# Weight sums by accumulating DMAs, activation sums on VectorE, and block products that alternate with tiles, in a two-layer Mamba-2 / HGRN2 trunk

## The chip, the cores and the metric

The kernel runs on one core of one Trainium2 chip. The metric is the device time of one execution in microseconds (us). PE is the matrix engine TensorE (PEld its weight loads), DVE is VectorE, ACT is ScalarE, POOL is GpSimd, and SP is SyncE, whose queue issues the DMAs.

## The reference, cut to what matters

Two layers work on 512 tokens of width 1024 in fp32. Each layer has a token mixer (Mamba-2 SSD in layer 0, HGRN2 in layer 1), a squared-ReLU MLP of width 4096, two layer norms and a gated per-layer embedding. The change lies in the MLPs.

```python
def sq_relu_mlp(h, w1, w2):
    a = jax.nn.relu(h @ w1)
    return (a * a) @ w2

for i in range(DEPTH):                                   # DEPTH = 2
    mix = ssd_mixer(x, ...) if i % 2 == 0 else hgrn2_mixer(x, ...)
    h = layer_norm(ALPHA * x + mix, ln_g[i, 0], ln_b[i, 0])
    h = layer_norm(ALPHA * h + sq_relu_mlp(h, w1[i], w2[i]), ln_g[i, 1], ln_b[i, 1])
    x = h + sigmoid(h @ ple_w_gate[i]) * (p[i] @ ple_w_proj[i])
```

Here `h` is 512 x 1024, `w1` 1024 x 4096 and `w2` 4096 x 1024.

## The kernel before

**Precision.** Every large product is made of three matmuls on operands that are split into a high and a low part: `split` makes `whi` on ACT (L110, a cast to fp32r) and `wlo` on DVE (L112, the difference), and `mm3` (L116 to L118) adds high x high, high x low and low x high into one bank. `unit` loads one 128x1024 tile of weights (512 KB) into one of the three `raw` buffers by a DMA on SP's queue and splits it; there are five buffers each for `whi` and `wlo`.

**First half of an MLP.** `hidden(g, p)` makes four tiles of relu(h @ w1)^2, each with one unit of `w1` and 24 matmuls of 512 columns (in the very first four tiles 48 matmuls of 256): ACT takes relu (L369) and square (L370) from the bank. `half_blocks` then prepares half of the blocks of group `g`: the tiles' quarters `a11`, `a12`, `a21`, `a22` and four sums of them, `s1` to `s4`. Seven of these eight are stored as a high part (ACT, L263) and a low part (DVE, L264); the four sums are made on POOL.

**Second half.** The product with `w2` is made by a seven-product scheme for 2 x 2 blocks (Strassen-Winograd) in four groups of 1024 hidden units. `block_product` (`o0` to `o3`) loads the group's eight tiles of `w2` into the buffers `r` (L287), makes eight sums of them on POOL (L290, L292, L321, L325), splits fourteen tiles, and runs seven products of 24 matmuls, each for two row tiles `c`. Products that belong to the same output share a pair of banks (`py0`, `py1` for `x`; two banks `pj` for `y` and `z`): after each product DVE adds the bank into `acc` (L314, L316), and the next product into that bank waits for this.

The order of the pieces is written out by hand:

```python
ORDER = "h00 h01 h10 o0 h11 h20 o1 h21 h30 h31 o2 o3".split()
```

so the last two block products follow each other. In `o3` the next layer norm's chunks (`after(0)` to `after(3)`) are called between the products. The scheduler orders the instructions of each engine by program order and priority when the program is built: `tc.high_priority(offset=SUMS)` moves the loads and sums of `w2` ahead by 220 places, `LEAD` the units by 100. Each engine then runs its list strictly in order.

**Around it.** Ahead of the MLP, `norm` adds the mixer's output into `acc` (L223), normalizes it (L189 to L197) and transposes it on PE (L206). Behind it, the gate takes `h @ ple_w_gate` and `p @ ple_w_proj` per row tile, with a sigmoid buffer `sg` (L410 to L414).

Of the kernel before, what the change touches and what calls it, by code (L numbers as in the profile page):

```python
# [26 lines left out]
LEAD = 100  # L27
RAWS = 3
FIRST = 1000

ORDER = "h00 h01 h10 o0 h11 h20 o1 h21 h30 h31 o2 o3".split()
SUMS = 220

JOBS = "q2 q3 v1 q4 q5 v2 q6 q7 v3 o".split()
FILL = (2.0, 1.0, 1.3, 1.6, 2.3, 2.8)
# [7 lines left out]
def trunk(ctx: ExitStack, tc, a):  # L43
    nc = tc.nc
    pool = lambda name, bufs, **kw: ctx.enter_context(tc.tile_pool(name=name, bufs=bufs, **kw))
    cpool = pool("consts", 1)
    raws = pool("raws", RAWS)
    whip = pool("whip", 5)
    wlop = pool("wlop", 5)
    b8 = pool("b8", 9)  # L50
    accp = pool("accp", 1)
    w4 = pool("w4", 2)
    sm = pool("sm", 2)
    psj = pool("psj", 4, space=PSUM)
    pst = pool("pst", 1, space=PSUM)
    psy = pool("psy", 1, space=PSUM)
# [8 lines left out]
    def mk(p, shape, tag, dt=F32, **kw):  # L65
        return p.tile(list(shape), dt, tag=tag, name=nm(tag), **kw)

    def f32(t):
        return t.bitcast(F32)

    two = dict(xs=2, sz=2, cv=2, cm=2, cbm=2)
    mlp = dict(r=10, blk=2, sg=2)
    bufs = dict(ssd=dict(two, ss=2), mlp0=mlp, hgrn=dict(two, xs=4, sz=4, cv=4, y=2, pv=2, btok=2), mlp1=mlp)
    phase = []

    def begin(name):

        if phase:
            phase[1].__exit__(None, None, None)
            phase.clear()  # L80
        phase.append(tc.tile_pool(name=name, bufs=1, reuse_waits="tile"))
        phase.append(phase[0].__enter__())
        phase.reverse()
        phase.append(bufs[name])

    def tmp(tag, shape, dt=F32):
        return mk(phase[0], shape, tag, dt, bufs=phase[2].get(tag, 1))

    def bank(p, tag):
        return mk(p, [P, T], tag)  # L90
# [8 lines left out]
    def unit(src, lead=LEAD):  # L99
        n = src.shape[1]  # L100
        with tc.high_priority(offset=lead):
            raw = mk(raws, [P, 1024], "raw")
            nc.sync.dma_start(raw[:, :n], src)
        return split(raw[:, :n], lead)

    def split(f, lead=LEAD):
        n = f.shape[1]
        with tc.high_priority(offset=lead):
            hi = mk(whip, [P, 1024], "whi", F32R)
            nc.scalar.copy(hi[:, :n], f)  # L110
            lo = mk(wlop, [P, 1024], "wlo", F32R)
            nc.vector.tensor_sub(lo[:, :n], f, f32(hi[:, :n]))  # L112
        return hi, lo
# [19 lines left out]
    def project(src, xs, ps, m=P, tok=slice(0, T)):  # L133

        hi, lo = src
        for k in range(8):
            c = slice(k * m, (k + 1) * m)
            mm3(ps[:m, tok], hi[:, c], lo[:, c], xs.h(k, tok), xs.l(k, tok), k == 0, k == 7)


    begin("ssd")
    acc = mk(accp, [P, NCH, D], "acc")
    xraw = acc.rearrange("p c (h t) -> p (c h) t", h=2)
# [111 lines left out]

    def half_blocks(blk, z0, z1, p):

        ks = slice(2 * p, 2 * p + 2)
        a11, a12, a21, a22 = z0[:, :, :256], z1[:, :, :256], z0[:, :, 256:], z1[:, :, 256:]

        def put(name, f):
            hi, lo = blk[name][:, 0, ks, :], blk[name][:, 1, ks, :]
            nc.scalar.copy(hi, f)  # L263
            nc.vector.tensor_sub(lo, f, f32(hi))  # L264

        put("a22", a22)
        put("a11", a11)
        put("a12", a12)
        nc.gpsimd.tensor_add(a22, a21, a22)
        put("s1", a22)  # L270
        nc.gpsimd.tensor_sub(a21, a11, a21)
        put("s3", a21)
        nc.gpsimd.tensor_sub(a11, a22, a11)
        put("s2", a11)
        nc.gpsimd.tensor_sub(a12, a12, a11)
        put("s4", a12)

    def block_product(w, blk, first, after=None):


        with tc.high_priority(offset=SUMS):
            raw = {}
            for i, j in ((0, 0), (0, 1), (1, 1), (1, 0)):
                raw[i, j] = []
                for u in range(2):
                    raw[i, j].append(tmp("r", [P, 1024]))
                    nc.sync.dma_start(raw[i, j][u], w[i][j][u])  # L287
            t1, t2, t3, t4 = raw[0, 1], [tmp("r", [P, 1024]) for _ in range(2)], raw[0, 0], raw[1, 0]
            for u in range(2):
                nc.gpsimd.tensor_sub(t1[u], raw[0, 1][u], raw[0, 0][u])  # L290
            for u in range(2):
                nc.gpsimd.tensor_sub(t2[u], raw[1, 1][u], t1[u])  # L292
        seen = set() if first else {(i, j) for i in range(2) for j in range(2)}
        banks = {}

        def product(x, f, name, start, i, j, then=None):
            us = [split(v) for v in f]
            if then is not None:
                with tc.high_priority(offset=LEAD):
                    then()  # L300
            if start:
                banks[name] = [bank(psy, "py%d" % c) if name == "x" else bank(psj, "pj") for c in range(2)]
            t = blk[x]
            for c in range(2):
                ps = banks[name][c]
                sl = slice(c * P, (c + 1) * P)
                for k in range(4):
                    hi, lo = us[k // 2]
                    ks = slice((k % 2) * 512, (k % 2 + 1) * 512)
                    w_ = hi[:, ks], lo[:, ks]  # L310
                    mm3(ps, t[:, 0, k, sl], t[:, 1, k, sl], *w_, start and k == 0, k == 3, skip_group_check=True)
                d = acc[:, 2 * i + c, j * 512 : (j + 1) * 512]
                if (i, j) in seen:
                    nc.vector.tensor_add(d, ps, d)  # L314
                else:
                    nc.vector.scalar_tensor_tensor(d, d, ALPHA, ps, ALU.mult, ALU.add)  # L316
            seen.add((i, j))

        def sums3():
            for u in range(2):  # L320
                nc.gpsimd.tensor_sub(t3[u], t2[u], raw[0, 0][u])  # L321

        def sums4():
            for u in range(2):
                nc.gpsimd.tensor_sub(t4[u], raw[1, 0][u], t2[u])  # L325

        product("a11", raw[0, 0], "x", True, 0, 0, sums3)
        product("a12", raw[1, 0], "z", True, 0, 0, sums4)
        product("s2", t2, "x", False, 1, 0)
        p7 = lambda: product("s3", t3, "y", True, 1, 1)  # L330
        p5 = lambda: product("s1", t1, "x", False, 1, 1)
        p4 = lambda: product("a22", t4, "y", False, 1, 0)
        p3 = lambda: product("s4", raw[1, 1], "x", False, 0, 1)
        if after is None:
            for f in (p7, p5, p4, p3):
                f()
        else:
            p5(), p3(), after(0), after(1)
            p7(), p4(), after(2), after(3)

    def mlp_and_gate(layer, h_s, last):

        w1, w2 = a[f"w1_{layer}"], a[f"w2_{layer}"]
        blocks = {}

        def hidden(g, p):
            if p == 0:
                names = ("a11", "a12", "a22", "s1", "s2", "s3", "s4")
                blocks[g] = {
                    n: tmp("blk", [P, 2, 4, 256], F32R) if n in ("s3", "s4") else mk(b8, [P, 2, 4, 256], "b8", F32R)  # L350
                    for n in names
                }
            tiles = [4 * (2 * g + r) + 2 * p + i for r in range(2) for i in range(2)]
            us = []
            if g == p == 0:
                for m in tiles:
                    us.append((unit(w1[m]), bank(psj, "pj")))
                    project(us[-1][0], h_s, us[-1][1], tok=slice(0, 256))
            zs = []
            for r in range(2):  # L360
                z = mk(w4, [P, 2, T], "ab"[r])
                for i in range(2):
                    if us:
                        u, ps = us[2 * r + i]
                        project(u, h_s, ps, tok=slice(256, 512))
                    else:
                        ps = bank(psj, "pj")
                        project(unit(w1[tiles[2 * r + i]]), h_s, ps)
                    nc.scalar.activation(z[:, i], ps, AF.Relu)  # L369
                nc.scalar.activation(z, z, AF.Square)  # L370
                zs.append(z)
            half_blocks(blocks[g], *zs, p)

        for op in ORDER:
            g = int(op[1])
            if op[0] == "h":
                hidden(g, int(op[2]))
            else:
                if g == 3:
                    h_s, after = norm(2 * layer + 1)  # L380
                w = [[[w2[8 * g + 4 * i + 2 * j + u] for u in range(2)] for j in range(2)] for i in range(2)]
                block_product(w, blocks.pop(g), g == 0, after if g == 3 else None)

        p_s = (mk(w4, [P, 2, T], "a", F32R), mk(w4, [P, 2, T], "b", F32R))
        praw = mk(w4, [P, 2, T], "a")
# [654 lines left out]
```

## Time and profile before

| | |
|---|---|
| time, median of 3 runs (lowest to highest) | 1508.86 us (1508.42 to 1509.92) |
| the profiled execution's own time | 1508.68 us |
| its span, first to last instruction | 1506.9 us |
| mean granted clock of PE | 0.993 |
| busy: PE / DVE / ACT / POOL | 1470.1 / 1101.0 / 723.5 / 274.8 us |
| MLP of layer 0, with gate | about 395 to 810 us of the span |
| MLP of layer 1, with gate | about 1100 us to the end |

A row of the time line reads: start in us from the span's start, duration in us, engine, line, operation, out<-in, shapes, and in brackets how long the engine was idle before it and what ended that wait. A row of a group has behind the bar the busy time in us, the mean duration of one in ns, and the idle time before them. In the rows of stretches, each engine has its busy time and the number of its instructions; behind them stand the granted clock of PE as a share of full speed, the mean busy share of the DMA engines and GB/s. Matmuls are pipelined: a single row's duration is longer than the distance between two starts, and PE's pace is read from the starts.

### The profile page before, as it was taken

Reading aid. Unit: us, or ns where it says so; the run is one execution under the profiler, and the core shown is the slowest. Engines: PE = TensorE matmul, PEld = TensorE weight load, DVE = VectorE, ACT = ScalarE, POOL = GpSimd, SP = SyncE. Lnnn points to the kernel's source line nnn. Section 1 sums busy time; section 2 is a strip of 40 time slices with the busy share of each in tenths; the row PEclk is TensorE's granted clock in tenths of the full one; section 3 lists DMA queues with packets and bytes.
Section 4 is the critical chain, followed back from the end, with each engine's and each line's share of the span. In section 5 each row is a group of like instructions: output and inputs, shape, how many; then the busy total and the mean of one; then the engine's idle time right before and its main releaser. Section 6 shows DMA issues by size and latency. Waiting matters only on the chain.

```text
span 1506.9 us, 19584 instructions
## 1 busy us (share of the span) xinstructions
PE 1470.1 (98%) x7720; PEld 1222.1 (81%) x7720; DVE 1101.0 (73%) x1544; ACT 723.5 (48%) x1020; POOL 274.8 (18%) x136
## 2 busy tenths in 40 slices
PE   8999999999999999998999999999999999999898
PEld 5888888888888888876778998988798888887677
DVE  7998686787777586398944866769766958549883
ACT  6776455563364454453534453543245454444342
POOL 0000000001145251363000000000215435235200
PEclk9999999999999999998999999999999999999999
DMA  6433323234223324130223212222431423314022
GB/s 247 155 112 107 112 93 109 99 118 175 88 69 112 112 89 137 55 126 28 81 70 112 94 61 71 72 70 84 154 112 43 134 90 112 127 42 140 14 85 70
DMA packets 41612, 149.93 MB, mean 99 GB/s; under 512 B 4624, under 2 KB 5136, under 8 KB 41392
## 3 DMA queue, kind: packets, MB, share of 16 engines
q1 hardware_dynamic: 41520, 148.67, 29.4%
q8 instruction: 61, 1.00, 0.3%
q14 instruction: 31, 0.25, 0.1%
HBM read 146.49 MB, written 2.16 MB: 99 GB/s over the span
## 4 chain that ended last, share of the span: by engine, by line
PE 88%; DVE 9%; DMA 2%; ACT 1%; issue 0%; POOL 0%; SPq 0%; ACTq 0%; DVEq 0%
PE pj L116 23%; PE pj L117 23%; PE pj L118 23%; DVE wlo L112 4%; PE py L116 3%; PE py L118 3%; PE py L117 3%; DVE b L264 2%; PE py L778 1%; PE py L587 1%; DVE acc L314 1%; PE pm L557 1%; PE pt L206 1%; PE py L592 1%; DMA a<-in_pT 1%; DVE blk L264 1%
## 5 line engine op out<-in xcount | busy, mean ns | idle before, releaser
L116 PE MATMUL pj<-b,whi 128*128 128x512 f32 (+1 forms) x1024 | 392.0, 383 | 1.2 <-ACT whi L110 1.2
L118 PE MATMUL pj<-b,wlo 128*128 128x512 f32 (+1 forms) x1024 | 388.1, 379 | 0.0
L117 PE MATMUL pj<-b,whi 128*128 128x512 f32 (+1 forms) x1024 | 387.5, 379 | 0.0
L112 DVE TENSOR_TENSOR wlo<-raw,whi 128x1024 fp32r<-128x1024 f32 x180 | 230.4, 1281 | 110.5 <-ACT whi L110 109.6
L110 ACT CAST whi<-raw 128x1024 fp32r<-128x1024 f32 x180 | 188.8, 1050 | 237.3 <-PE pj L117 129.5
L112 DVE TENSOR_TENSOR wlo<-r,whi 128x1024 fp32r<-128x1024 f32 x112 | 194.0, 1737 | 89.7 <-ACT whi L110 89.7
L116 PE MATMUL pj<-whi,b 128*128 128x512 f32 (+1 forms) x712 | 252.3, 355 | 0.5 <-ACT sg L410 0.5
L117 PE MATMUL pj<-wlo,b 128*128 128x512 f32 (+1 forms) x712 | 249.6, 351 | 0.8 <-DVE wlo L112 0.8
L118 PE MATMUL pj<-whi,b 128*128 128x512 f32 (+1 forms) x712 | 250.1, 351 | 0.0
L116 PEld LDWEIGHTS pj<-b,whi 128*128 128x128 f32 x1024 | 192.9, 188 | 36.7 <-ACT whi L110 2.9
L118 PEld LDWEIGHTS pj<-b,wlo 128*128 128x128 f32 x1024 | 192.7, 188 | 35.9 <-DVE wlo L112 1.3
L117 PEld LDWEIGHTS pj<-b,whi 128*128 128x128 f32 x1024 | 192.9, 188 | 34.0 <-issue 1.9
L110 ACT CAST whi<-r 128x1024 fp32r<-128x1024 f32 x112 | 116.8, 1048 | 189.6 <-PE pj L117 60.9
L290 POOL TENSOR_TENSOR r<-r,r 128x1024 f32<-128x1024 f32 x16 | 45.1, 2826 | 767.6 <-DMA r<-in_w 760.0
L117 PEld LDWEIGHTS pj<-wlo,b 128*128 128x128 f32 x712 | 134.7, 189 | 18.4 <-DVE wlo L112 2.0
L116 PEld LDWEIGHTS pj<-whi,b 128*128 128x128 f32 x712 | 134.7, 189 | 17.7 <-ACT sg L410 0.7
L118 PEld LDWEIGHTS pj<-whi,b 128*128 128x128 f32 x712 | 134.5, 189 | 17.0 <-issue 0.2
L116 PE MATMUL py<-whi,b 128*128 128x512 f32 x192 | 77.2, 402 | 15.5 <-DVE acc L314 15.5
L118 PE MATMUL py<-whi,b 128*128 128x512 f32 x224 | 88.8, 398 | 0.0
L264 DVE TENSOR_TENSOR b<-b,b 128x512 fp32r<-128x512 f32 x48 | 62.7, 1322 | 21.5 <-ACT b L263 21.3
L117 PE MATMUL py<-wlo,b 128*128 128x512 f32 x192 | 76.6, 399 | 0.6 <-DVE wlo L112 0.6
L321 POOL TENSOR_TENSOR r<-r,r 128x1024 f32<-128x1024 f32 x16 | 39.8, 2485 | 125.0 <-DVE wlo L112 125.0
(217 smaller groups left out, 2064.3 us busy)
## 6 DMA issues: line engine op xcount, KB each, us to landing
raw<-in_w SPq DMA_DIRECT2D x64, 512.0 KB, 3.6
r<-in_w SPq DMA_DIRECT2D x64, 512.0 KB, 3.7
raw<-in_wssd SPq DMA_DIRECT2D x40, 512.0 KB, 3.6
a<-csd SPq DMA_DIRECT2D x16, 512.0 KB, 3.9
raw<-in_wso SPq DMA_DIRECT2D x16, 512.0 KB, 3.5
raw<-in_wg SPq DMA_DIRECT2D x16, 512.0 KB, 3.6
raw<-in_whvg SPq DMA_DIRECT2D x16, 512.0 KB, 3.5
raw<-in_whq SPq DMA_DIRECT2D x16, 512.0 KB, 3.6
```

Of the source, the lines that this page charges most:

```text
L110: nc.scalar.copy(hi[:, :n], f)
L112: nc.vector.tensor_sub(lo[:, :n], f, f32(hi[:, :n]))
L116: nc.tensor.matmul(out, sh, mh, start=start, stop=False, **kw)
L117: nc.tensor.matmul(out, sh, ml, start=False, stop=False, **kw)
L118: nc.tensor.matmul(out, sl, mh, start=False, stop=stop, **kw)
L206: nc.tensor.transpose(pt[:, j * P : (j + 1) * P], src[:, k * P : (k + 1) * P], ident)
L264: nc.vector.tensor_sub(lo, f, f32(hi))
L290: nc.gpsimd.tensor_sub(t1[u], raw[0, 1][u], raw[0, 0][u])
L314: nc.vector.tensor_add(d, ps, d)
L321: nc.gpsimd.tensor_sub(t3[u], t2[u], raw[0, 0][u])
L557: nc.tensor.matmul(pst_[:, c * P : (c + 1) * P], btok[:, c, :], xw[:, c].rearrange("p h q -> p (h q)"), start=True, stop=True)
L587: nc.tensor.matmul(yd[64 * r : 64 * r + 64, sl], xdt[:, 2 * c + r, :], m[:, r, sl], start=True, stop=True)
```

## The change

The order of the MLP is now written as periods of tiles (T) and products (Q), with the four tiles of `hidden` and the seven products of `block_product` made into generators. Period 0 has eight tiles. In periods 1 to 3 the eight tiles of group `g` alternate with the seven products of group `g - 1`. The last period has the seven products of group 3.

The block sums of `w2` are made by DMAs that add (`accum_op=ALU.add`, issued by POOL, SBUF to SBUF, 512 KB each) on top of a loaded tile; where a negative sign is needed, the tile is loaded into a `raw` buffer and negated on ACT. The three tiles of `w2` that are used unchanged are loaded by `unit`, so that each group has 16 loads on SP's queue where it had 8, and 8 accumulating DMAs where it had 8 sums on POOL. The four sums of activations move to DVE, and the low parts of the half-blocks become scalar-tensor-tensor operations, since two of the blocks are stored with their sign changed. The buffers `sg` go from two to one, POOL's descriptor memory grows from 1024 to 4096 bytes, and a small `pad` tile is added. The matmuls are the same in number and shape.

```diff
-ORDER = "h00 h01 h10 o0 h11 h20 o1 h21 h30 h31 o2 o3".split()
-SUMS = 220
+PERIODS = ("TTTTTTTT",) + 3 * ("TTQTQTQTQTQTQTQ",) + ("QQQQQQQ",)
+SUMS = 300
...
-    mlp = dict(r=10, blk=2, sg=2)
+    mlp = dict(r=10, blk=2)
...
     def half_blocks(blk, z0, z1, p):
...
-        def put(name, f):
+        def put(name, f, sign=1.0):
             hi, lo = blk[name][:, 0, ks, :], blk[name][:, 1, ks, :]
-            nc.scalar.copy(hi, f)
-            nc.vector.tensor_sub(lo, f, f32(hi))
-
-        put("a22", a22)
+            nc.scalar.activation(hi, f, AF.Copy, scale=sign)
+            nc.vector.scalar_tensor_tensor(lo, f, sign, f32(hi), ALU.mult, ALU.subtract)
+
         put("a11", a11)
+        put("a22", a22, -1.0)
+        nc.vector.tensor_add(a22, a21, a22)
         put("a12", a12)
-        nc.gpsimd.tensor_add(a22, a21, a22)
-        put("s1", a22)
-        nc.gpsimd.tensor_sub(a21, a11, a21)
+        nc.vector.tensor_sub(a21, a11, a21)
+        nc.vector.tensor_sub(a11, a22, a11)
+        nc.vector.tensor_sub(a12, a12, a11)
+        put("s2", a11)
         put("s3", a21)
-        nc.gpsimd.tensor_sub(a11, a22, a11)
-        put("s2", a11)
-        nc.gpsimd.tensor_sub(a12, a12, a11)
+        put("s1", a22, -1.0)
         put("s4", a12)
+    def weight_sums(w):
+        t = [[None, None] for _ in range(5)]
+        def add(i, u, src):
+            nc.gpsimd.dma_start(t[i][u], src, accum_op=ALU.add)
+        def put(i, u, src, neg):
+            t[i][u] = tmp("r", [P, 1024])
+            if not neg:
+                nc.sync.dma_start(t[i][u], src)
+                return
+            raw = mk(raws, [P, 1024], "raw")
+            nc.sync.dma_start(raw, src)
+            nc.scalar.mul(t[i][u], raw, -1.0)
+        with tc.high_priority(offset=SUMS):
+            for u in range(2):
+                put(0, u, w[0][1][u], True)
+                put(3, u, w[1][1][u], False)
+                add(3, u, t[0][u])
+                put(2, u, w[0][0][u], False)
+                add(2, u, t[3][u])
+            for u in range(2):
+                put(1, u, w[0][0][u], False)
+                add(1, u, t[0][u])
+                put(4, u, w[1][0][u], True)
+                add(4, u, t[2][u])
+        return t[1:]
...
-        product("a11", raw[0, 0], "x", True, 0, 0, sums3)
-        product("a12", raw[1, 0], "z", True, 0, 0, sums4)
-        product("s2", t2, "x", False, 1, 0)
+        p1 = lambda: product("a11", w[0][0], "x", True, 0, 0)
+        p2 = lambda: product("a12", w[1][0], "z", True, 0, 0)
+        p6 = lambda: product("s2", t2, "x", False, 1, 0)
         p7 = lambda: product("s3", t3, "y", True, 1, 1)
         p5 = lambda: product("s1", t1, "x", False, 1, 1)
         p4 = lambda: product("a22", t4, "y", False, 1, 0)
-        p3 = lambda: product("s4", raw[1, 1], "x", False, 0, 1)
+        p3 = lambda: product("s4", w[1][1], "x", False, 0, 1)
...
+        for f in (p1, p2, p6, p5, p3, p7, p4) if after else (p1, p2, p6, p7, p5, p4, p3):
+            f()
...
+            yield
...
+        for g, period in enumerate(PERIODS):
+            if g < 4:
+                tiles = hidden(g)
+            if g > 0:
...
+                products = block_product(w, blocks.pop(g - 1), g == 1, after if g == 4 else None)
+            for op in period:
+                next(tiles if op == "T" else products)
...
-    nc = _bacc.Bacc("TRN2", target_bir_lowering=False, num_devices=1, dynamic_dma_scratch_size=1024)
+    nc = _bacc.Bacc("TRN2", target_bir_lowering=False, num_devices=1, dynamic_dma_scratch_size=4096)
```

The lines of the changed kernel stand two to three places lower up to the MLP's functions: the casts and splits of weights are L111 and L113 there, the matmuls of `mm3` L117 to L119, the layer norm's last step L199, its transposes L208, the sums into `acc` L333 and L335, the adding DMAs L286.

More of the change, by code (lines that the diff above doesn't have):

```diff
@@ L53, in trunk @@
     sm = pool("sm", 2)
+    pad = pool("pad", 1)
     psj = pool("psj", 4, space=PSUM)
@@ L138, in project @@
             mm3(ps[:m, tok], hi[:, c], lo[:, c], xs.h(k, tok), xs.l(k, tok), k == 0, k == 7)
+    nc.gpsimd.memset(mk(pad, [P, 16], "pad"), 0.0)
     begin("ssd")
@@ L276, in half_blocks @@
         put("s4", a12)
-    def block_product(w, blk, first, after=None):
[L281 to L292, printed above, removed]
+    def weight_sums(w):
[23 more added lines that the diff above has]
+        return t[1:]
@@ L293, in block_product, with product @@
+    def block_product(w, blk, first, after=None):
+        t1, t2, t3, t4 = weight_sums(w)
         seen = set() if first else {(i, j) for i in range(2) for j in range(2)}
         banks = {}
[L296 to L300, printed above, removed]
+        def product(x, f, name, start, i, j):
+            us = [split(v) if f in (t1, t2, t3, t4) else unit(v) for v in f]
@@ L317, in product @@
             seen.add((i, j))
[L319 to L325, printed above, removed]
-        product("a11", raw[0, 0], "x", True, 0, 0, sums3)
-        product("a12", raw[1, 0], "z", True, 0, 0, sums4)
-        product("s2", t2, "x", False, 1, 0)
+        p1 = lambda: product("a11", w[0][0], "x", True, 0, 0)
+        p2 = lambda: product("a12", w[1][0], "z", True, 0, 0)
+        p6 = lambda: product("s2", t2, "x", False, 1, 0)
         p7 = lambda: product("s3", t3, "y", True, 1, 1)
@@ L332, in block_product @@
         p4 = lambda: product("a22", t4, "y", False, 1, 0)
-        p3 = lambda: product("s4", raw[1, 1], "x", False, 0, 1)
[L334 to L339, printed above, removed]
+        p3 = lambda: product("s4", w[1][1], "x", False, 0, 1)
+        for f in (p1, p2, p6, p5, p3, p7, p4) if after else (p1, p2, p6, p7, p5, p4, p3):
+            f()
+            if after and f is p3:
+                after(0), after(1)
+            if after and f is p4:
+                after(2), after(3)
+            yield
     def mlp_and_gate(layer, h_s, last):
@@ L344, in mlp_and_gate @@
         blocks = {}
[L346 to L379, printed above, removed]
+        def hidden(g):
+            names = ("a11", "a12", "a22", "s1", "s2", "s3", "s4")
+            blocks[g] = {
+                n: tmp("blk", [P, 2, 4, 256], F32R) if n in ("s3", "s4") else mk(b8, [P, 2, 4, 256], "b8", F32R)
+                for n in names
+            }
+            for p in range(2):
+                tiles = [4 * (2 * g + r) + 2 * p + i for r in range(2) for i in range(2)]
+                us = []
+                if g == p == 0:
+                    for m in tiles:
+                        us.append((unit(w1[m]), bank(psj, "pj")))
+                        project(us[-1][0], h_s, us[-1][1], tok=slice(0, 256))
+                zs = []
+                for r in range(2):
+                    z = mk(w4, [P, 2, T], "ab"[r])
+                    for i in range(2):
+                        if us:
+                            u, ps = us[2 * r + i]
+                            project(u, h_s, ps, tok=slice(256, 512))
+                        else:
+                            ps = bank(psj, "pj")
+                            project(unit(w1[tiles[2 * r + i]]), h_s, ps)
+                        nc.scalar.activation(z[:, i], ps, AF.Relu)
+                        if i == 1:
+                            nc.scalar.activation(z, z, AF.Square)
+                            zs.append(z)
+                            if r == 1:
+                                half_blocks(blocks[g], *zs, p)
+                        yield
@@ L380, in mlp_and_gate @@
+        for g, period in enumerate(PERIODS):
+            if g < 4:
+                tiles = hidden(g)
+            if g > 0:
+                if g == 4:
                     h_s, after = norm(2 * layer + 1)
-                w = [[[w2[8 * g + 4 * i + 2 * j + u] for u in range(2)] for j in range(2)] for i in range(2)]
-                block_product(w, blocks.pop(g), g == 0, after if g == 3 else None)
+                w = [[[w2[8 * g - 8 + 4 * i + 2 * j + u] for u in range(2)] for j in range(2)] for i in range(2)]
+                products = block_product(w, blocks.pop(g - 1), g == 1, after if g == 4 else None)
+            for op in period:
+                next(tiles if op == "T" else products)
```

## The prediction

> **What bounds the kernel now.** I read the page first, then the list of waits of the matrix engine (PE), then the busy times by stretch, and last the instructions in order of time in the worst stretches.
>
> ```profile
> span 1506.9 us, 19584 instructions
> PE 1470.1 (98%) x7720; PEld 1222.1 (81%) x7720; DVE 1101.0 (73%) x1544; ACT 723.5 (48%) x1020; POOL 274.8 (18%) x136
> ...
> PE py L116 <- DVE acc L314: 15.5, 5, 6.3
> PE pj L117 <- DVE wlo L112: 4.4, 4, 1.8
> PE pt L206 <- DVE acc L197: 3.3, 2, 1.8
> ...
> core 0: us, PE busy (x) PEld busy (x) DVE busy (x) ACT busy (x) POOL busy (x), PEclk, DMA share, GB/s
> 430.00:635.00 205.00, 205.00 (x902) 169.16 (x902) 133.36 (x114) 97.86 (x122) 80.47 (x39) 1.00 0.30 96
> 635.00:680.00 45.00, 43.22 (x183) 35.08 (x182) 40.38 (x33) 22.46 (x29) 25.83 (x14) 0.96 0.35 116
> 680.00:735.00 55.00, 47.38 (x198) 37.28 (x197) 49.45 (x50) 18.24 (x22) 12.06 (x5) 0.91 0.09 30
> 1345.00:1388.00 43.00, 40.25 (x175) 32.27 (x174) 40.00 (x33) 22.15 (x29) 24.10 (x12) 1.00 0.37 121
> 1388.00:1440.00 52.00, 44.10 (x186) 35.24 (x185) 46.45 (x48) 17.96 (x21) 12.24 (x5) 0.93 0.07 21
> ```
>
> The reader is to see that PE is the limit and that the diff leaves its matmuls alone, so only PE's holes can be won. In the body of an MLP (430 to 635) there are none. They lie where the block products `o2` and `o3` follow each other without tiles of the first half between them: 1.78 + 7.62 + 2.75 + 7.90 = 20.05 us idle in four stretches, with VectorE (DVE) busy nine tenths of them and the granted clock below 1.
>
> ```profile
> 676.61 3.08 DVE L112 TENSOR_TENSOR wlo<-r,whi 128x1024 fp32r<-128x1024 f32 x1
> 680.22 3.10 DVE L112 TENSOR_TENSOR wlo<-r,whi 128x1024 fp32r<-128x1024 f32 x1
> 683.84 3.09 DVE L112 TENSOR_TENSOR wlo<-r,whi 128x1024 fp32r<-128x1024 f32 x1
> ...
> 702.59 1.22 DVE L112 TENSOR_TENSOR wlo<-r,whi 128x1024 fp32r<-128x1024 f32 x1
> 703.73 0.68 DVE L314 TENSOR_TENSOR acc<-pj,acc 128x512 f32<-128x512 f32 x1
> ...
> 676.22 2.39 POOL L292 TENSOR_TENSOR r<-r,r 128x1024 f32<-128x1024 f32 x1 [7.62 <-DVE wlo L112]
> 679.83 2.41 POOL L292 TENSOR_TENSOR r<-r,r 128x1024 f32<-128x1024 f32 x1 [1.22 <-issue]
> 683.46 2.39 POOL L321 TENSOR_TENSOR r<-r,r 128x1024 f32<-128x1024 f32 x1 [1.23 <-DVE wlo L112]
> ...
> 684.56 0.39 PE L118 MATMUL py<-whi,blk 128*128 128x512 f32 x1
> 691.24 0.77 PE L116 MATMUL py<-whi,b 128*128 128x512 f32 x1 [6.29 <-DVE acc L314]
> 691.81 0.63 PE L117 MATMUL py<-wlo,b 128*128 128x512 f32 x1
> 692.23 0.63 PE L118 MATMUL py<-whi,b 128*128 128x512 f32 x1
> ```
>
> The cause is in these rows. A weight split (L112) takes 1.22 us while GpSimd (POOL) is quiet and 3.1 us, from start to start 3.6, while a sum of weights runs there. Behind it in DVE's queue stands the sum into `acc` (L314) that releases the bank `py`, and PE stands 6.29 us for it. After that PE's starts are 0.42 us apart, where rows at full clock (below) are 0.23 apart.
>
> **The change part by part.** All sums are against the profiled execution's own 1508.68 us (span 1506.9 and 1.8 around it), which is 0.2 under the median of 1508.86.
>
> *POOL's arithmetic goes.* In the four stretches the idle of 20.05 us is charged to DVE. The clock that is missing there is 0.04 x 45 + 0.09 x 55 + 0.07 x 52 = 10.4 us of full speed, part of which fell into the idle itself; I take 6 (bounds 0 and 10.4). The alternation also spreads `o2`'s DVE work, so I remove all of 26. A second place is the layer norm ahead of each MLP:
>
> ```profile
> 371.80 5.72 POOL L290 TENSOR_TENSOR r<-r,r 128x1024 f32<-128x1024 f32 x2 [370.39 <-DMA r<-in_w]
> ...
> 376.12 2.49 DVE L196 SCALAR_TENSOR_TENSOR acc<-acc,lnmv,a 128x1024 f32<-128x1024 f32 x1
> 379.85 2.09 DVE L197 SCALAR_TENSOR_TENSOR acc<-acc,lnrs,b 128x1024 f32<-128x1024 f32 x1
> ...
> 385.98 1.27 DVE L196 SCALAR_TENSOR_TENSOR acc<-acc,lnmv,a 128x1024 f32<-128x1024 f32 x1
> ```
>
> The first two run beside POOL's early sums and are 1.2 and 0.8 longer than the third. In the new order the weight sums of the first block come after the first tiles, so these 2.0 us go, and with them the waits of L206 on L197: 3.3 us, of which I take 3.
>
> *DVE and ScalarE (ACT) get POOL's work.* Rows for it:
>
> ```profile
> L316 DVE SCALAR_TENSOR_TENSOR acc<-acc,py 128x512 f32<-128x512 f32 x12 | 8.1, 678 | 0.8 <-PE py L118 0.8
> ...
> L370 ACT ACTIVATE b<-b 128x1024 f32<-128x1024 f32 x16 | 17.0, 1064 | 0.5
> L110 ACT CAST whi<-r 128x1024 fp32r<-128x1024 f32 x112 | 116.8, 1048 | 189.6 <-PE pj L117 60.9 <-PE py L118 54.4 <-issue 46.4
> L263 ACT CAST b<-b 128x512 fp32r<-128x512 f32 x48 | 29.0, 620 | 37.4 <-POOL b L269 30.1 <-PE pj L117 4.5 <-PE py L118 2.5
> ...
> raw<-in_w SPq DMA_DIRECT2D x64, 512.0 KB, 3.6
> ...
> 659.99 0.40 PE L117 MATMUL pj<-wlo,blk 128*128 128x512 f32 x1
> 660.23 0.39 PE L118 MATMUL pj<-whi,blk 128*128 128x512 f32 x1
> 660.46 0.40 PE L116 MATMUL pj<-whi,blk 128*128 128x512 f32 x1
> 662.63 0.50 PE L117 MATMUL pj<-wlo,blk 128*128 128x512 f32 x1 [1.78 <-DVE wlo L112]
> 662.97 0.43 PE L118 MATMUL pj<-whi,blk 128*128 128x512 f32 x1
> 663.21 0.62 PE L116 MATMUL pj<-whi,blk 128*128 128x512 f32 x1
> 663.63 0.63 PE L117 MATMUL pj<-wlo,blk 128*128 128x512 f32 x1
> ```
>
> A tile (T) or a product (Q) is 24 matmuls, 0.227 us apart: 5.44 us. A middle period has 8 T and 7 Q, 81.7 us of PE. DVE in it: 22 splits x 1.22, 14 sums into `acc` x 0.68, and two half-blocks of 11 operations x 0.68 (the four sums that were POOL's among them): 26.8 + 9.5 + 15.0 = 51. ACT: 22 casts and 4 negations x 1.05, 4 squares x 1.06, 8 relus and 14 casts of half-blocks x 0.62: 45. Both lie beside PE. Were that cover gone, as in the last block, they cost what the next part says. Each period also has 24 loads where there were 16; SP issues them in one queue, behind loads that wait for one of the three `raw` buffers.
>
> *The end of a middle period.* I followed the built program's order with these durations, time 0 being the end of the period's last tile. The half-blocks' last casts wait for Q7 (end 5.4). The first product of the next period has two tiles ahead of it and starts at 16.3; its weights are split at 13.8 and 15.0. So nothing, with 2.5 us to spare.
>
> *The last block* (seven Q behind each other) has no tiles ahead. On ACT, relu, square and two negations (0.6 + 1.1 + 2 x 1.05) stand ahead of the first weight cast, and the load of the second weight waits for the `raw` buffer that the first of these negations frees, at 2.7; it lands at 2.7 + 3.6 = 6.3 and is split at 9.7, behind half-block work on both engines. The first product's first half should run from 5.4 to 8.2 and ends at 10.9: 2.7 lost. The built order then runs the second product to 16.5, and the first one's second half needs bank `py1`, whose last sum into `acc` stands on DVE behind four puts and three splits of half-block and weights and ends at 19.7: 3.2 lost. From there DVE keeps ahead (splits 1.22 and sums 0.68 against 5.44 per product), so 5.9 a layer, 11.8 in all. With no slip on ACT it would be 0, with loads a third slower and a half-block later 20.
>
> *The clock after such holes.* An idle of 1.78 us at 660.5 is followed by starts 0.42 apart. I add 1 us a layer, 2 in all (bounds 0 and 5). The Trainium skill, "TensorE: Matmul & The Clock Gate", section on the HAM clock gate, has the clock halve after an idle window of about 3.4 us; here 1.78 was enough, so the row decides; by the page the sum would be 2 us less.
>
> *The accumulating DMAs.* The trace of before has none. A plain load of the same 512 KB lands in 3.6 us; an addition reads its target too, and I take 5, with 3.6 and three loads' time, 10.8, as bounds. POOL issues one, waits for it and issues the next: two follow each other before t2 is ready. In a middle period t2's second half starts from the negation at 2.7, and ACT comes to its cast at about 22.7, when the next period's first product has ended; in the last block the same slack is 21. So up to 10 us each they cost nothing. Gate buffers `sg` go from two to one: sigmoid, product and sum (0.6 + 0.7 + 0.7) fit in the 30 matmuls, 6.8 us, between two of them: 0.
>
> Sum: 1508.7 - 20 - 6 - 3 + 11.8 + 2 = 1493.5; I say 1494.
>
> **The rivals.**
>
> *Late weight sums (slower).* ACT's queue is in order, so a t2 that isn't there blocks the relus and every later weight behind it, and PE a little after. Beyond 10 us for one accumulating DMA each period loses twice the excess, in three places of each MLP: 12 us for each us. From 11.3 us on the whole gain is gone; at 12 it is 1518, at 14 it is 1542. For it: no row bounds the DMA from above, and POOL, which makes them ready, shared something with DVE in the rows at 676 to 684. Against it: 30% DMA share. Chance 0.22.
>
> *The last block loses twice what I found.* DVE was nine tenths busy there before; with holes of 12 us a layer and a clock of 2.5 us each, 1508.7 - 29 + 24 + 5 = 1509; over the way there, 1500 to 1509. Chance 0.14. One way into it: the new splits of the half-blocks are scalar-tensor-tensor operations on two fp32 operands of SBUF, and if these ran at half speed, 0.6 more for seven of them ahead of that sum into `acc` would make 4.2 a layer, 1502. L196 takes 1.27 for 1024 elements and the plain L112 1.22, so I give it 0.03 of the 0.14. The Trainium skill, "Vector Engine (DVE) Microarchitecture Reference", section "Points that are easy to get wrong", states that halving; the L196 row contradicts it.
>
> *The change does not free DVE.* If POOL's making of descriptors slows DVE as its arithmetic did, holes stay where they were and the last block's come on top: 1508.7 - 3 + 5 to 10, 1506 to 1516. Against it: 64 short issues stand where POOL's 136 instructions were busy for 274.8 us. Chance 0.10.
>
> **How the numbers follow.** My own case has 0.54: 1494, with 1484 (no holes in the last block) to 1502. Two in ten may fall outside, mostly late sums far above: the range is 1484 to 1520. Within 0.2% means 3 us, about what a measurement of this kernel can tell. Faster: 0.54, 0.09 of the last block's case and 0.01: 0.64. Same: 0.05 and 0.02, 0.07. Slower: 0.22 and 0.07: 0.29.
>
> **What would show it.** Right: no busy POOL, splits at L113 of 1.2 us throughout, no wait of PE in the middle periods, and in the last block two waits, on a split of the first product's second weight and on a sum into `acc`, some 3 us each; L208's wait on L199 gone. Wrong: a wait of ACT on an accumulated `r` with an issue-to-landing time over 10 us (late sums); splits over 2 us (DVE not freed); waits over 5 us in the last block.

## The result: 2.4% slower, and the profile after

The changed kernel takes 1545.58 us (median of 4 runs, 1544.37 to 1549.89), the kernel before on the same chip 1509.39 (1508.42 to 1513.29): a ratio of 1.024, 95% interval 1.0213 to 1.0267. The forecast was 1494, with 1520 as the upper end. The profiled execution took 1545.44 us, 36.8 more than the profiled 1508.68 of before.

From the page of the changed kernel, parts 1, 3 and 6 (DMA queues have packets, MB and share of 16 engines' time; issues have KB each and the median us to landing):

```profile
span 1543.7 us, 19742 instructions
PE 1489.9 (97%) x7720; PEld 1227.9 (80%) x7720; DVE 1018.6 (66%) x1608; ACT 753.6 (49%) x1052; POOL 56.6 (4%) x73
...
q1 hardware_dynamic: 50736, 182.23, 33.8%
q0 software_dynamic: 9216, 33.56, 11.1%
...
raw<-in_w SPq DMA_DIRECT2D x144, 512.0 KB, 6.4
r<-r POOLq DMA_DIRECT2D x64, 512.0 KB, 10.7
r<-in_w SPq DMA_DIRECT2D x48, 512.0 KB, 8.4
```

POOL is quiet and DVE has 82 us less to do, as the change intends. But PE is busy 20 us longer with the same matmuls (most of it in stretches at half clock) and idle 17 us longer. What has become dear stands in part 6: a load into a `raw` buffer lands in 6.4 us where it took 3.6. From part 3, one adding DMA holds the 16 engines for 11.1% of 1543.7 us / 64 = 2.7 us; one load (182.23 MB are 348 pieces of 512 KB) for 33.8% / 348 = 1.5 us.

Groups of DVE, then the waits of PE (us in total, times, longest):

```profile
L113 DVE TENSOR_TENSOR wlo<-raw,whi 128x1024 fp32r<-128x1024 f32 x228 | 278.6, 1222 | 232.5 <-ACT whi L111 231.6
...
L267 DVE SCALAR_TENSOR_TENSOR b<-b,b 128x512 fp32r<-128x512 f32 x48 | 32.3, 687 | 13.5 <-ACT b L266 13.5
```

```profile
PE py L117 <- ACT whi L111: 19.2, 12, 3.7
PE py L118 <- DVE wlo L113: 9.0, 12, 1.2
PE py L117 <- DVE acc L333: 6.0, 2, 3.0
...
PE pj L118 <- DVE wlo L113: 3.7, 8, 0.8
```

Every split runs at 1.22 us. L208's wait on L199 is gone. The predicted wait on a sum into `acc` is there once in each MLP, 3.0 us. The rest is new: 12 times a cast of weights is late for a product into `py`, 19.2 us, and a late split follows each time. Where this happens, by stretch (columns as in the prediction's table; DMA share and GB/s last):

```profile
530.00:540.00 10.00, 7.12 (x18) 4.83 (x19) 3.68 (x3) 4.86 (x6) 3.49 (x4) 0.66 1.01 215
...
690.00:700.00 10.00, 6.06 (x25) 4.33 (x23) 2.67 (x4) 6.34 (x9) 2.60 (x3) 1.00 1.05 295
700.00:710.00 10.00, 6.05 (x12) 3.52 (x13) 4.44 (x7) 3.39 (x5) 0.88 (x2) 0.52 1.06 278
710.00:725.00 15.00, 10.32 (x32) 7.14 (x33) 11.36 (x14) 5.45 (x7) 1.76 (x2) 0.84 0.92 270
...
1335.00:1350.00 15.00, 12.71 (x53) 9.43 (x52) 6.31 (x8) 7.05 (x10) 4.16 (x5) 1.00 1.05 293
```

The first and last row are ends of middle periods (one of each layer), the three others the last block of layer 0. The DMA share is near 1 in all of them; in the worst stretches of the kernel before it was 0.07 to 0.37. Except at the wait on `acc`, DVE does not hold PE up here (in the first row it is busy 3.7 of 10 us); data is late. The chain of waits (start, us, what) names it, in two middle periods and then through the last block of layer 0:

```profile
521.22 12.02 DMA raw<-in_w
...
609.82 12.01 DMA raw<-in_w
...
681.31 14.98 DMA raw<-in_w
...
696.38 1.06 ACT r L295
...
699.32 1.23 DVE wlo L113
...
700.57 12.26 DMA raw<-in_w
...
712.85 1.05 ACT whi L111
...
713.95 0.80 PE pj L117
714.75 0.43 PE pj L118
```

In the last block a load of 14.98 us ends in a negation (L295). Only then does ACT come to the first product's first weight, whose split (L113) frees a `raw` buffer, and only into that can the load of the second product's second weight be issued: another 12.26 us, where such a load took 3.6 in the kernel before. Behind the hole PE starts matmuls 0.43 us apart instead of 0.23.

Summed from the distances between matmul starts, each against the 0.227 us of full clock, holes and half-clock together, the two MLPs, each with the layer norms at its two ends, lose 68.5 us where they lost 34.1: 34.4 of the 36.8. The slow starts alone went from 8.1 to 22.6. Another 1.7 arise ahead of the first layer norm, at the program's start, where the change moves no matmul.

### The profile page after: what moved, and what is told of

It is laid out like the page before. It is cut to its first block, busy times and chain, and to the rows that moved or that the text cites. A ratio compares the mean times of both kernels' runs of the same rounds, so it can differ in the third digit from the quotient of the medians.

```text
span 1543.7 us, 19742 instructions
## 1 busy us (share of the span) xinstructions
PE 1489.9 (97%) x7720; PEld 1227.9 (80%) x7720; DVE 1018.6 (66%) x1608; ACT 753.6 (49%) x1052; POOL 56.6 (4%) x73
## 3 DMA queue, kind: packets, MB, share of 16 engines
q1 hardware_dynamic: 50736, 182.23, 33.8%
q0 software_dynamic: 9216, 33.56, 11.1%
## 4 chain that ended last, share of the span: by engine, by line
PE 78%; DMA 14%; DVE 4%; ACT 3%; issue 1%; SPq 0%; ACTq 0%
PE pj L117 20%; PE pj L118 20%; PE pj L119 19%; DMA raw<-in_w 13%; PE py L118 3%; PE py L117 3%; PE py L119 3%; DVE wlo L113 2%; ACT whi L111 2%; PE py L794 1%; PE py L603 1%; PE pm L573 1%; PE pt L208 1%; PE py L608 1%; ACT r L295 1%; DVE b L267 1%
## 5 line engine op out<-in xcount | busy, mean ns | idle before, releaser
L113 DVE TENSOR_TENSOR wlo<-raw,whi 128x1024 fp32r<-128x1024 f32 x228 | 278.6, 1222 | 232.5 <-ACT whi L111 231.6
L111 ACT CAST whi<-raw 128x1024 fp32r<-128x1024 f32 x228 | 238.8, 1048 | 333.3 <-PE pj L118 109.2
L117 PE MATMUL pj<-b,whi 128*128 128x512 f32 (+1 forms) x1024 | 392.1, 383 | 1.8 <-ACT whi L111 1.8
L119 PE MATMUL pj<-b,wlo 128*128 128x512 f32 (+1 forms) x1024 | 388.5, 380 | 0.0
L117 PE MATMUL pj<-whi,b 128*128 128x512 f32 (+1 forms) x712 | 253.9, 358 | 2.2 <-ACT whi L111 1.5
L119 PE MATMUL pj<-whi,b 128*128 128x512 f32 (+1 forms) x712 | 251.3, 353 | 0.0
L117 PEld LDWEIGHTS pj<-b,whi 128*128 128x128 f32 x1024 | 193.0, 189 | 37.8 <-ACT whi L111 4.8
L119 PEld LDWEIGHTS pj<-b,wlo 128*128 128x128 f32 x1024 | 192.9, 188 | 35.8 <-DVE wlo L113 1.4
L117 PEld LDWEIGHTS pj<-whi,b 128*128 128x128 f32 x712 | 135.5, 191 | 22.4 <-ACT whi L111 4.6
L119 PEld LDWEIGHTS pj<-whi,b 128*128 128x128 f32 x712 | 135.3, 190 | 16.8 <-issue 0.2
L111 ACT CAST whi<-r 128x1024 fp32r<-128x1024 f32 x64 | 66.8, 1044 | 90.1 <-PE pj L118 62.4
L286 POOL DMA_DIRECT2D r<-r x64 | 55.7, 950 | 1377.9 <-ACT b L266 1078.0
L113 DVE TENSOR_TENSOR wlo<-r,whi 128x1024 fp32r<-128x1024 f32 x64 | 78.1, 1221 | 42.3 <-ACT whi L111 42.2
L117 PE MATMUL py<-whi,b 128*128 128x512 f32 x192 | 81.5, 424 | 25.1 <-ACT whi L111 19.2
L119 PE MATMUL py<-whi,b 128*128 128x512 f32 x224 | 91.9, 412 | 0.0
L118 PE MATMUL py<-wlo,b 128*128 128x512 f32 x192 | 81.6, 425 | 9.0 <-DVE wlo L113 9.0
L117 PEld LDWEIGHTS py<-whi,b 128*128 128x128 f32 x192 | 38.7, 202 | 39.7 <-ACT whi L111 24.9
L508 DVE SCALAR_TENSOR_TENSOR cv<-pj,cst,cv 128x511 f32<-128x511 f32 (+2 forms) x72 | 53.4, 744 | 5.8 <-ACT cv L505 5.2
## 6 DMA issues: line engine op xcount, KB each, us to landing
r<-r POOLq DMA_DIRECT2D x64, 512.0 KB, 10.7
```

The source lines that it names most:

```text
L117: nc.tensor.matmul(out, sh, mh, start=start, stop=False, **kw)
L118: nc.tensor.matmul(out, sh, ml, start=False, stop=False, **kw)
L119: nc.tensor.matmul(out, sl, mh, start=False, stop=stop, **kw)
L286: nc.gpsimd.dma_start(t[i][u], src, accum_op=ALU.add)
L508: nc.vector.scalar_tensor_tensor(cv[:, d:], ps[:, : T - d], convw[:, i, k : k + 1], cv[:, d:], ALU.mult, ALU.add)
```

## The experiments

Two theories were tested against each other at first. A: the adding DMAs and the loads together fill the DMA engines around each period's end. B: the loads stand in SP's queue behind negated tiles that need one of three `raw` buffers, whatever the adds do. The ratios are those to the kernel before on the same chip (about 1512 us there). In e3, e4 and e7 the signs of two stored blocks do not match the sums, and e1 and e6 leave the sums out, so that the outputs of these five are not the reference's; number and shape of the operations are as described.

**e1: no adding DMAs.**

```diff
-            nc.gpsimd.dma_start(t[i][u], src, accum_op=ALU.add)
+            pass
```

> The changed kernel without its 64 accumulating DMAs (the products use unsummed weights; loads, negations, order and matmuls stay). In the changed kernel the accumulating queue holds the DMA engines for 11.1% of 1543.7 us = 171 us, 2.7 us each, and the raw loads land in 6.4 us where they took 3.6. Theory A (the adding DMAs and the loads together saturate the DMA engines around each end of a period, so that the first products' weights land late): the raw loads land in under 4.5 us, the waits on whi and wlo into py (28 us) fall under 8 us, time 1495 to 1510. Theory B (the loads wait in SP's queue behind the negated loads for one of three raw buffers, whatever the adds do): those waits stay above 20 us, time 1535 to 1545.

Measured: 1494.83 us, ratio 0.9897 (0.9877 to 0.9918). The DMAs of its last block in layer 0, 657 to 697 us, and behind them those of the corresponding 40 us of the changed kernel, 672 to 712:

```profile
q1 hardware_dynamic: 2880, 10.49, 71.9%
...
raw<-in_w SPq DMA_DIRECT2D x10, 512.0 KB, 4.4
```

```profile
q1 hardware_dynamic: 2212, 8.09, 54.7%
q0 software_dynamic: 829, 3.07, 38.4%
...
raw<-in_w SPq DMA_DIRECT2D x10, 512.0 KB, 12.0
r<-r POOLq DMA_DIRECT2D x8, 512.0 KB, 11.1
```

With the adds, the same ten loads into `raw` land in 12.0 us instead of 4.4: the adds take 38.4% of the engines' time there. The waits at the ends of the middle periods are gone in e1, and of the 28.2 us that PE waits for weights into `py` 4.5 are left. The burst of loads is still there: the ten loads for the sums of the last block are issued between 660.1 and 668.2, shortly ahead of the end of the last tile at 675.4, as in the changed kernel. So nothing but the adds is taken out of it. A alone explains this run; the time is 0.2 us under the lower end that was given for A. The Trainium skill, "DMA: Bandwidth & Descriptors", section "Queues, rings and completion order", says that each DMA engine takes turns between the queues it has work for, packet by packet; the two shares of 54.7% and 38.4% in one stretch agree with that: neither queue is shut out, and both are slow.

**e2: negate in place.**

```diff
-            raw = mk(raws, [P, 1024], "raw")
-            nc.sync.dma_start(raw, src)
-            nc.scalar.mul(t[i][u], raw, -1.0)
+            nc.sync.dma_start(t[i][u], src)
+            nc.scalar.mul(t[i][u], t[i][u], -1.0)
```

> The changed kernel, with the negated tiles loaded straight into their r buffer and negated there, so that they take no raw buffer and the loads of the products' own weights no longer wait for one behind them. Theory A (DMA engines saturated): the raw loads still take over 5.5 us and the time stays within 1530 to 1550. Theory B (raw buffers and queue order): the waits at the period ends and most of the last block's weight waits go, time 1500 to 1515.

Measured: 1519.13 us, 1.0047 (1.0033 to 1.0062), between the two forecasts; the `raw` loads land in 4.1 us, against what A says. The waits of PE, then one of ACT, say why:

```profile
PE pt L208 <- DVE b L212: 31.6, 4, 15.3
...
PE py L117 <- DVE acc L332: 1.9, 2, 1.0
...
ACT r L294 <- DMA r<-in_w: 107.0, 24, 14.1
```

All 64 adds and all loads are still there, but the products of the MLPs no longer wait for late weights, and an adding DMA lands in 5.6 us (10.7 in the changed kernel). In their place stands a new wait of 31.6 us: the scheduler put the first block's negations ahead of the layer norm's copies in ACT's list, and ACT stands at loads that have not landed. Neither A nor B holds alone.

**e5: in place from the second block on** (the first block's negations go through `raw`, as in the changed kernel).

> The changed kernel with in-place negation from the second block of each MLP on; in the first block the negated tiles go through raw buffers as in the changed kernel. The run with in-place negation everywhere had no waits on weights at the period ends but two new ones of 14.3 and 15.4 us in the layer norms, where ACT stood at a negation whose load had not landed. Theory AB (late weights need both: sum loads held back by the raw buffers into one burst, and adding DMAs in that burst): the layer norms' waits go too and all 64 adding DMAs stay, 1486 to 1496. If the in-place gain came from elsewhere (the adding DMAs as such cost), 1505 or more.

Measured: 1496.14 us, 0.989 (0.9875 to 0.9905), with all the adds, 0.1 us above the range that theory AB gave. Its stretch 640 to 700, and its waits of PE:

```profile
q1 hardware_dynamic: 2488, 9.01, 44.6%
q0 software_dynamic: 864, 3.15, 28.2%
...
raw<-in_w SPq DMA_DIRECT2D x8, 512.0 KB, 4.0
r<-r POOLq DMA_DIRECT2D x6, 512.0 KB, 5.3
```

```profile
PE pj L117 <- ACT whi L111: 5.5, 3, 2.3
...
PE py L117 <- DVE acc L337: 1.9, 2, 1.0
```

SP's queue shows what moved. Rows of its time line, changed kernel first, then e5:

```profile
674.66 0.33 SPq L294 DMA_DIRECT2D raw<-in_w  x1
...
676.99 0.33 SPq L294 DMA_DIRECT2D raw<-in_w  x1
677.42 2.37 SPq L291 DMA_DIRECT2D r<-in_w  x5
679.89 1.75 SPq L294 DMA_DIRECT2D raw<-in_w  x2
681.78 0.55 SPq L104 DMA_DIRECT2D raw<-in_w  x1
683.26 0.33 SPq L291 DMA_DIRECT2D r<-in_w  x1
```

```profile
641.45 0.33 SPq L291 DMA_DIRECT2D r<-in_w  x1
...
652.33 0.33 SPq L294 DMA_DIRECT2D r<-in_w  x1
660.55 0.33 SPq L291 DMA_DIRECT2D r<-in_w  x1
...
662.16 0.55 SPq L294 DMA_DIRECT2D r<-in_w  x1
```

In the changed kernel the ten loads for the sums of the last block are all issued between 674.7 and 683.3, in the last 15 us ahead of the end of the period's last tile (690.0): the first of them needs a `raw` buffer, which the split that ends at 674.6 frees, and the others are queued behind it. In e5 such loads leave one by one as buffers `r` come free; the last one is issued at 662.2, 21 us ahead of that end (683.0 there). So the cause is both halves together: the `raw` buffers press sixteen loads and eight adds into the stretch in which the first products' weights must come, and with the adds the engines cannot serve that stretch in time. Taking away either half brings the time to 0.99. No run gives the loads more `raw` buffers, which would be a third way to test it.

**e6: copies in place of adds** (`accum_op` left out).

> The changed kernel with each adding DMA made a plain copy of the same 512 KB between the same buffers (the sums are left out). In the changed kernel one adding DMA holds 16 engines for 2.7 us (11.1% of 1543.7 us / 64) and a load for 1.5 us. If the adding itself is dear (it reads its target too), a copy takes about 1.5 us of the engines, the burst shortens by about 8 x 1.2 us = 10 us and the time lies between the run without adds and the changed kernel, 1500 to 1525. If the bytes or descriptors alone count, the share of the queue stays near 11% and the time at 1535 to 1548.

Measured: 1506.73 us, 0.9961 (0.9946 to 0.9976).

```profile
q0 software_dynamic: 9216, 33.56, 5.7%
```

The same 33.56 MB hold the engines for 5.7% of 1505.2 us / 64 = 1.34 us each, half of an add's 2.7. So the addition itself doubles the price, and the time falls between e1 and the changed kernel, as it should when engine time in the burst is what counts.

**e3 and e4: the new order without DMA sums.** The eight loads and eight sums of the kernel before, on POOL (e3) or DVE (e4), with the new order and the activation sums on DVE.

> The changed kernel's order and its activation sums on DVE, with the weight sums made on POOL from eight loads as in the kernel before (no negations, no adding DMAs). Theory A and theory B both: no waits at the ends of the middle periods; the wait on a sum into acc in the last block returns as a POOL effect, with splits of 3.1 us beside POOL. Before lost about 14.5 us in the o2/o3 stretch of each MLP, of which o2's part goes with the alternation: 1495 to 1512. If the alternation itself is what costs (rival C: seven products in a row without tiles lose 15 us or more whatever makes the sums), 1520 or more.

> As the run with POOL's sums, but the weight sums on DVE (64 x 1.2 us = 78 us more on DVE, no POOL arithmetic in the MLPs, no adding DMAs, eight loads a period). Theory A and B: the removed 29 us plus 4 at the layer norms come off, and the last block costs about the predicted 6 to 10 us a layer: 1485 to 1500, faster than both kernels. Rival C (the last block in a row costs 15 us a layer anyway): 1510 or more.

Measured: 1497.78 us, 0.9911 (0.9886 to 0.9936), and 1492.35 us, 0.9879 (0.9859 to 0.9899), both as the theories say; rival C is out. **e10** repeats e4 with matching signs:

> The new order with all weight sums on DVE and the two blocks stored without change of sign, as that form of the sums needs. Same work as the earlier run with DVE's sums, which was at 0.9879 of the kernel before (0.9859 to 0.9899): 0.986 to 0.990. It shows what the new order gives with no adding DMA at all, against the run that has them in three blocks of four.

It took 1493.86 us, 0.9877 (0.9863 to 0.989), the same.

**e7: the old order with the DMA sums.**

> The kernel before with the weight sums of the change (negations through raw buffers, adding DMAs, 16 loads a block) in its old order, with the activation sums on POOL. Theory AB: the burst and the raw buffers are here as well, while DVE is freed of POOL's weight sums; the 20 us of idle in the o2/o3 stretches become waits on weights: 1505 to 1540. If the alternation is what makes the adding DMAs harmful, 1485 to 1500.

Measured: 1574.16 us, 1.0418 (1.0396 to 1.044), above both forecasts. Its waits of PE and ACT, and two rows of POOL:

```profile
PE py L116 <- DVE acc L330: 40.2, 8, 7.8
...
ACT b L263 <- POOL b L269: 46.3, 10, 9.0
```

```profile
671.29 0.86 POOL L283 DMA_DIRECT2D r<-r  x1 [10.79 <-issue]
671.85 1.59 POOL L269 TENSOR_TENSOR b<-a,b 128x512 f32<-128x512 f32 x1
```

Here the activation sums (L269) are still on POOL, in order behind an adding DMA that was issued only after 10.79 us of idling; casts, splits and at last the sums into `acc` follow late. So with the adding DMAs the activation sums could not stay on POOL. This run loses its time by another way than the changed kernel, so it does not show what the adding DMAs alone cost in the old order: no run has them there with the activation sums on DVE.

**e8: a longer tail.** The run with DVE's sums, with `TTQTTQTTQTTQQQQ` as the last period with tiles.

> The new order with the weight sums on DVE, and the last period with tiles written TTQTTQTTQTTQQQQ, so that three more products of group 2 stand between the last tile and the last block. In the run with DVE's sums each last block still had a wait of 3.25 us on a sum into acc and half-clock matmuls of 2.0 us behind it. If these come from the half-blocks' work on DVE ahead of the first products (the step the prediction gave for 3.2 us), they go: 1480 to 1489. If they come from the seven products in a row, 1490 to 1495.

Measured: 1494.7 us, 0.9879 (0.9863 to 0.9895): no gain. The 3.3 us wait on a sum into `acc` of each MLP stands there still, in front of a product into a bank `pj`. In layer 0 it begins 13 us behind the end of the last tile (17 in e4), when two products of group 2 are not yet done. So it follows the last tile, as the half-blocks' work does, and not the seven products in a row; but three products between do not cover it, and neither reading was right as a whole.

**e9: the first block's sums on DVE, the rest by DMA in place.**

> The changed kernel with in-place negation and adding DMAs in the second to fourth block of each MLP, and the first block's weight sums on DVE (eight loads, eight operations of 1.2 us). The run with in-place negation from the second block on still lost 4.4 us a layer (1.75 + 1.12 + 1.57) where the first block's negations went through raw buffers. If that is all that the first block costs, this takes 8 us off that run: 0.983 to 0.986 of the kernel before, 1484 to 1488. If DVE's sums beside the layer norm cost as much (1.57 + 0.84 at layer 0 in the run with all sums on DVE), 0.987 to 0.989.

Measured: 1494.23 us, 0.9885 (0.9867 to 0.9903). The expected 8 us did not come: weights of the second block are late instead (a hole of 3.5 us at 517), because ACT, which makes their high parts, stood for 8.2 and 7.2 us at two negations ahead of them whose loads had not landed (75.7 us in all over the kernel). An in-place negation needs no `raw` buffer; it stands early in ACT's list, and what is behind it waits.

**e11 and e12: the old order with sums on DVE.** In `half_blocks` (e12), and in `block_product` too (e11), `nc.gpsimd` becomes `nc.vector`.

> The kernel before in its old order, with the sums of weights and of activations on DVE and no arithmetic on POOL. If POOL's slowing of DVE (splits of 3.1 us instead of 1.2) is the main cause of the idle 20 us in the o2/o3 stretches, most of the gain comes without the new order: 1490 to 1500. If the alternation is what counts there, 1502 to 1512.

> The kernel before with only the four activation sums moved from POOL to DVE (0.68 us each, 32 half-blocks' worth in all), weight sums still on POOL, old order. If the weight sums on POOL do the slowing, nothing changes within 4 us: 1505 to 1513. If the activation sums on POOL hold up the half-blocks (the casts waited 30 us for POOL in the kernel before), 1495 to 1504.

Measured: e12 1502.1 us, 0.9932 (0.9918 to 0.9946); e11 1490.62 us (1489.77 to 1493.45), 0.9859 (0.9846 to 0.9873), the lowest time here, by little: e10, on the same chip, took 1493.86. First a wait of PE in e12, then two groups of DVE in e11:

```profile
PE py L116 <- DVE acc L314: 14.7, 6, 3.6
```

```profile
L112 DVE TENSOR_TENSOR wlo<-r,whi 128x1024 fp32r<-128x1024 f32 x112 | 136.1, 1221 | 80.4 <-ACT whi L110 79.5
...
L290 DVE TENSOR_TENSOR r<-r,r 128x1024 f32<-128x1024 f32 x16 | 19.5, 1218 | 1.4 <-DMA r<-in_w 1.4
```

In e11 DVE takes POOL's sums at 1.2 us each and is still less busy than in the kernel before (1087.0 against 1101.0 us), since its own operations no longer stretch. So the idle of the `o2`/`o3` stretches came from the sums on POOL; neither the new order nor a DMA is needed to remove it. e12 divides the 22.2 us that e11 gains on the 1512.81 of the kernel before there: the activation sums bring 10.7, as its second reading said, and with the weight sums still on POOL the splits of `r` take 1.6 us in the mean and the wait on `acc` is nearly what it was (15.5). Whether the activation sums cost by slowing DVE or by coming late themselves is not separated. The new order by itself changes little either way: with the weight sums on POOL 0.9911 (e3) against 0.9932 (e12), with all on DVE 0.9877 (e10) against 0.9859.

## Why the prediction was wrong, step by step

- **What is removed** (29 us with the layer norms): right. The MLPs lost 34.1 us before; of the 68.5 that they lose now, 2.6 lie outside the two places below, so at least 31.5 went. POOL's descriptors do not slow DVE (every split 1.22 us): the third rival is out. Its own sum was off: 1508.7 - 3 + 5 to 10 is 1511 to 1516, not 1506 to 1516.
- **DVE's and ACT's new work:** right. The scalar-tensor-tensor operations take 0.687 us, not twice that.
- **The end of a middle period, "nothing, with 2.5 us to spare":** wrong, and it cost 23.8 us (at the starts of periods 1 to 3: 1.2, 7.1, 6.2 in layer 0; 0.9, 4.0, 4.4 in layer 1). The loads of the first product's weights were taken at 3.6 us; the loads behind the waits of periods 2 and 3 took 12.0 in layer 0 and 9.1 to 11.4 in layer 1 (the chain of waits), 5.5 to 8.4 more, against 2.5 to spare. e1, without adds, has no such wait.
- **The last block, 11.8 us and 2 of clock:** 42.1 measured (20.8 and 21.3). The wait on the sum into `acc` was put at 3.2 a layer and is 3.16 by the starts. The other term, 2.7 for the second weight, rests on the same 3.6 us; that load took 10.9 and 11.7. The first weight, for which the forecast had no wait at all, landed only 7.6 us behind the last tile's end in layer 0, 15.8 after its issue. In e1 the last blocks lose 7.4 and 7.1, 14.5 in all against the forecast's 13.8. So the order of events was right, and the one duration put into it, that of a load, was wrong.
- **The adding DMAs:** here the reasoning failed. They were priced by when their own result is needed, with a threshold of 10 us. They landed in 10.7, a little over it, and ACT's list of waits names no accumulated `r`: that part held, and the rival "late weight sums" did not happen. What was left out is that they use the same 16 engines as the loads, and that the extra loads queue behind the `raw` buffers up to the period's end. The prediction noted both facts (24 loads where there were 16, one queue, three buffers; an addition reads its target too) and then used a load's duration from a trace without them. A sum over the stretch would have shown it: 16 loads of 1.5 and 8 adds of 2.7 are 46 us of all engines for each block, where the kernel before needs 8 x 1.5 = 12 beside its tiles. In the last block of layer 0 the engines were full from 674.7 to 722.1 (a share of 1.01 over 47 us).
- **The clock:** 2 us more were forecast beside 6 less; the slow starts grew by 14.5, as most of the new holes of a microsecond or more are followed by up to 4 us at half clock.
- **The rivals:** the second, a dearer last block, has one of the two places right, but its price (24 and 5) and its means were others. No rival had the loads late in the middle periods.

That e1 came to 1494.83, beside a forecast of 1494, says the same: the prediction describes this kernel with its adding DMAs at no cost to anything else. That all of the loss comes from burst and adds together is shown by e1 and e5; how it divides between the two is not, since each removes it nearly whole.

## What to carry to other kernels

Work that is handed to the DMA engines has two prices: when its result lands, and what it takes from the loads that share those engines; add up the engine time of all transfers in the tightest stretch, not over the span. When a load borrows a staging buffer, look at which loads stand behind it in the queue: a buffer that comes free late turns a steady stream into a burst. And where one engine slows another, first try the plain move (the same operations on the engine that was being slowed): here it gave the lowest time, in the old order, if by little.

## What the runs showed of the hardware that was not expected

An adding DMA of 512 KB between buffers of SBUF holds the 16 DMA engines for 2.7 us, a copy of the same size for 1.34, a load for 1.5. With the loads spread out (e2, e5) it lands in 5.6 us after issue, in the burst in 11.1. With the old order and all sums on DVE (e11), DVE did 64 more operations of 1.2 us and 64 of 0.7 and was busy 14 us less, since POOL's arithmetic, which had stretched its own, was gone.
